# Hybrid decoder layer on one core: gate and up with seven block products in place of eight for three of eight pairs of k tiles

## The chip, the cores and the metric

The kernel runs on one core of a Trainium2 chip. The metric is the device time of one execution in microseconds. One core has a matrix engine (TensorE, in the profile PE, its weight loads PEld), three engines for elementwise work (VectorE or DVE, ScalarE or ACT, GpSimd or POOL) and an engine that issues most transfers (SyncE, SP). Matrix results land in PSUM, eight banks of 512 float32 columns on each of 128 partitions.

## The reference, cut to what matters

256 tokens of width 2048 go through a SwiGLU half step (inner width 5632), a two-branch mixer and a second SwiGLU half step:

```python
def swiglu(h, w_gu, w_down):
    g, u = jnp.split(h @ w_gu, 2, axis=-1)
    return (jax.nn.silu(g) * u) @ w_down

x = x + 0.5 * swiglu(rms_norm(x, g_ffn1[l]), w_gu1[l], w_down1[l])
x = x + hybrid_mixer(rms_norm(x, g_mix[l]), w_in[l], ...)
x = x + 0.5 * swiglu(rms_norm(x, g_ffn2[l]), w_gu2[l], w_down2[l])
```

All data is float32. The change lies in the two SwiGLU steps.

## The kernel before

Every float32 operand of a large product is split into two float32r parts, hi and lo, by `split` (L93): ScalarE casts hi (L95), VectorE subtracts to get lo (L96). A product is the sum of hi·hi, hi·lo and lo·hi. The weights pass through a `Feed`: SyncE fetches groups of 128 x 2048 (1 MB) into three raw buffers, and parts of 128 x 1024 are split into three pairs of hi and lo buffers. A part may be split once the part three places ahead of it has been used by TensorE, so the split runs at most two parts ahead of the products. Each engine works its instructions off in the order in which the program emits them; nothing is reordered.

There are two forms of product. `by_column` (L192) keeps the weights stationary: for each k tile of 128 and each block of 128 columns, one matmul of whi with both parts of the activations side by side (512 columns, L207) and one of wlo with the hi part (256 columns, L209, L206). `by_token` (L169) keeps the activations stationary and streams the weights: three matmuls of 512 columns (L185 to L187) for each k tile and each half of 128 tokens. Gate and up use `by_column`, 44 tiles of 256 columns (128 of gate, 128 of up) in each SwiGLU step, 16 k tiles each; down uses `by_token`, in two halves of 22 k tiles.

The 1/rms of the tokens is not needed for the first products: it is applied to their results (`scaled`, L252 to L256, by `rows`). So the rms is computed beside the first tiles. `pending` holds work for TensorE that is run between parts (one item per part), `posts` work for ScalarE and VectorE that is run when a part is taken.

PSUM is given out in rotation: `ps_mm` has two buffers of two banks for results, `ps_t` two banks for transposes, `ps_a` two single banks for attention.

Of the kernel before, what the change touches and what calls it, by code (L numbers as in the profile page):

```python
# [12 lines left out]
F32 = mybir.dt.float32  # L13
# [12 lines left out]
HALVES = 2  # L26
FKT = DFF // P // HALVES
# [12 lines left out]
NCH = 512  # L40
ND = D // NCH
RAW = 4 * NCH
SUB = 2 * NCH
BUFS = 3
WAKE = 8
# [4 lines left out]
def hybrid_layer(ctx: ExitStack, tc: tile.TileContext, a: dict, out: bass.AP):  # L50
# [50 lines left out]
    def transpose4(srcs, name):  # L101
        """srcs[t]: [128 tokens, 256 columns] -> PSUM [128 columns, 2, 256 tokens]"""
# [14 lines left out]
    class Feed:  # L117
        """The weights in the order of their use: fetched in groups, split part by part, both ahead of the products"""

        def __init__(self):  # L120
            self.groups, self.parts = [], []
            self.fetched = self.split = self.taken = 0
            self.raw, self.ready = {}, {}

        def add(self, dram, width, cuts=None, on_fetch=None, on_split=None):
            """dram: [128, width]; cuts: the widths of the parts where each is fetched by itself"""
            for c0 in range(0, width, RAW):
                n = min(RAW, width - c0)
                g, o, ws, whole = len(self.groups), 0, [], not cuts
                while o < n:  # L130
                    w = cuts.pop(0) if cuts else min(SUB, n - o)
                    ws.append(w)
                    self.parts.append((g, o, w, c0 + o, on_split))
                    o += w
# [15 lines left out]

        def take(self):
            while self.split < min(self.taken + BUFS, len(self.parts)):
                i = self.split
                self.split += 1
                g, o, w, col, hook = self.parts[i]
                self.fetch(g + BUFS)
                hi = wsplit.tile([P, SUB], F32R, tag="hi", name="hi")
                lo = wsplit.tile([P, SUB], F32R, tag="lo", name="lo")
                split((hi[:, :w], lo[:, :w]), self.raw[g][:, o:o + w])
                if hook:  # L160
                    hook(col, w)
                self.ready[i] = hi, lo, w
# [6 lines left out]
    def by_token(x, kts, name, step, apart=False):  # L169
        """x @ w, the activations stationary; step takes PSUM [128 tokens, 512] for both token blocks"""  # L170
# [6 lines left out]
        while k0 < kts:  # L177
            hi, lo, w = feed.take()
# [11 lines left out]
        posts.append(lambda: step(ps))  # L190

    def by_column(x, kts, name, *steps):  # L192
        """(x @ w)^T, the weights stationary; steps take SBUF [128 columns, 2 column blocks, 256 tokens]"""
        ps = ps_mm.tile([P, 2, NCH], F32, tag="mm", name=name)
        k0 = 0
        while k0 < kts:
            hi, lo, w = feed.take()
# [27 lines left out]
    def rsqrt(v, shape, name):  # L225
        """1 / sqrt(v), refined once"""
# [10 lines left out]
    class Norm:  # L237
        """h: (x * gain)^T in two parts; rows: 1/rms of every token along the free dimension"""

        def __init__(self, which):  # L240
            self.which = which
            self.h = keep.tile([P, NKD, 2, S], F32R, tag="h", name=f"h{which}")
# [29 lines left out]

    class NormOfColumns(Norm):
        """x^T comes from DRAM"""

        def __init__(self, which, xT, pool):
# [3 lines left out]
            self.sq = [pool.tile([P, 4, S], F32, name=f"sq{i}") for i in range(3)]  # L280
            self.acc = pool.tile([P, 4, S], F32, name="acc")

        def fetch(self, col, w):
            ks = slice(col // (2 * P), (col + w) // (2 * P))
            nc.sync.dma_start(self.xT[:, ks], self.dram[:, ks])

        def parts(self, col, w):
            for k in range(col // (2 * P), (col + w) // (2 * P)):
                self.part(k, self.xT[:, k])

        def stats(self, c):
            x = self.xT[:, 4 * c:4 * c + 4]
            dst = self.sq[c - 1] if c else self.acc
# [40 lines left out]
    def add_ffn(w_gu, w_down, first=None):  # L334
        for half in range(HALVES):
            for c in range(FKT):
                w, hooks = w_gu[half * FKT + c], {}
                if first and half == 0 and c == 0:
                    ks = (1, 1, 2, 2, 2, 2, 2, 2, 2)
                    hooks = dict(cuts=[k * 2 * P for k in ks], on_fetch=first.fetch, on_split=first.parts)  # L340
                if first and half == 0 and c == 1:
                    hooks = dict(cuts=[k * 2 * P for k in (2, 2, 4)])
                feed.add(w, NKD * 2 * P, **hooks)
            for n in range(ND):
                feed.add(w_down[half, n], FKT * NCH)
# [13 lines left out]
    def ffn(norm, fpool, first=None, after=None, late=(), out_rows=None):  # L359
        for half in range(HALVES):  # L360
            last = half == HALVES - 1
            act = fpool.tile([P, FKT, 2, S], F32R, tag="act", name="act")

            def gated(c, act=act):
                def gate(s):
                    sg = work.tile([P, S], F32, tag="sg", name="sg")
                    nc.scalar.activation(sg, s[:, 0], AF.Silu)
                    nc.vector.tensor_tensor(s[:, 0], s[:, 1], sg, op=ALU.mult)

                def parts(s):  # L370
                    split((act[:, c, 0], act[:, c, 1]), s[:, 0])

                return norm.scaled, gate, parts

            c0 = first(gated) if first and half == 0 else 0
            for c in range(c0, FKT):
                steps = gated(c)
                if half == 0 and c == 0:
# [358 lines left out]
```

## Time and profile before

| what | value |
|---|---|
| time before, median of 3 runs | 2096.28 us (2095.21 to 2096.97) |
| span of the profiled execution | 2094.5 us |
| TensorE busy | 2084.7 us, 100% of the span |
| VectorE busy | 1238.6 us, 59% |
| ScalarE busy | 982.9 us, 47% |
| weights read | 386 MB, 185 GB/s over the span |

The profile describes one execution; its span runs from the first to the last instruction, and no other time of that execution is listed beside it, so the span is what the profile gives. A busy TensorE is one that always has a matmul in its pipeline; the time that one costs is read from the distance of two starts, since each is shown longer than that (0.39 us shown, 0.23 us from start to start).

### The profile page before, as it was taken

The page shows a single profiled execution, that of the slowest core. Times are in us where ns is not written, and L with a number is a line of the kernel's source. Part 1 is how long each engine was busy: PE and PEld are TensorE (multiplying, and loading weights), DVE is VectorE, ACT ScalarE, POOL GpSimd, SP SyncE. Part 2 cuts the span into 40 slices and gives each one's busy share as a digit, 9 for nine tenths or more (in the row PEclk, how much of TensorE's full clock was granted, in tenths as well). Part 3 has the DMA queues.
Part 4 walks back from the last instruction along what each step waited for, and adds up shares of the span by engine and source line. Part 5 has one row for each costly group of instructions (what it writes and reads, how often), then busy time and mean ns, then how long its engine had stood idle before and what let it go on. Part 6 is the DMA issues. An engine that isn't in the chain of part 4 may idle for free.

```text
span 2094.5 us, 27027 instructions
## 1 busy us (share of the span) xinstructions
PE 2084.7 (100%) x10972; PEld 1771.2 (85%) x10972; DVE 1238.6 (59%) x1404; ACT 982.9 (47%) x1273; POOL 66.2 (3%) x55
## 2 busy tenths in 40 slices
PE   9999999999999999999999999999999999999999
PEld 8888888888888888877888888888888888888887
DVE  7656644556655555568666665565665445665544
ACT  6544433444444444445544444554444334444433
POOL 2000000000000000621000000000000000000000
PEclk9999999999999999999999999999999999999999
DMA  7655555655555555443555555555555555555564
GB/s 247 235 184 188 192 181 183 200 186 193 184 183 179 191 191 193 152 141 134 185 183 195 186 192 191 181 181 183 191 189 172 201 193 190 190 181 185 184 215 140
DMA packets 59246, 389.86 MB, mean 186 GB/s; under 512 B 7024, under 2 KB 7664, under 8 KB 13936
## 3 DMA queue, kind: packets, MB, share of 16 engines
q1 hardware_dynamic: 58976, 388.10, 55.3%
q8 instruction: 86, 1.41, 0.3%
q14 instruction: 40, 0.33, 0.0%
q10 hardware_dynamic: 144, 0.02, 0.0%
HBM read 386.00 MB, written 2.10 MB: 185 GB/s over the span
## 4 chain that ended last, share of the span: by engine, by line
PE 97%; POOL 1%; DMA 0%; DVE 0%; issue 0%; ACT 0%; SPq 0%; POOLq 0%; DVEq 0%; ACTq 0%
PE gu L207 31%; PE gu L209 15%; PE dn L187 8%; PE dn L186 8%; PE dn L185 8%; PE gate L207 6%; PE yo L207 3%; PE gate L209 3%; PE xc L207 2%; PE bg L207 2%; PE o L185 1%; PE o L187 1%; PE o L186 1%; PE yo L209 1%; PE qkv L187 1%; PE qkv L186 1%
## 5 line engine op out<-in xcount | busy, mean ns | idle before, releaser
L96 DVE TENSOR_TENSOR lo<-raw,hi 128x1024 fp32r<-128x1024 f32 (+1 forms) x734 | 912.7, 1244 | 793.8 <-ACT hi L95 784.5
L95 ACT CAST hi<-raw 128x1024 fp32r<-128x1024 f32 (+1 forms) x734 | 766.4, 1044 | 1003.1 <-PE gu L207 490.9
L207 PE MATMUL gu<-h,hi 128*128 128x512 f32 x2816 | 989.5, 398 | 1.0 <-DVE h L248 1.0
L209 PE MATMUL gu<-h,lo 128*128 128x256 f32 x2640 | 742.3, 281 | 0.4 <-DVE lo L96 0.4
L207 PEld LDWEIGHTS gu<-h,hi 128*128 128x128 f32 x2816 | 524.1, 188 | 123.7 <-DVE h L248 1.8
L209 PEld LDWEIGHTS gu<-h,lo 128*128 128x128 f32 x2640 | 499.4, 189 | 4.7 <-DVE lo L96 1.1
L187 PE MATMUL dn<-hi,act 128*128 128x512 f32 x704 | 277.1, 394 | 0.0
L186 PE MATMUL dn<-lo,act 128*128 128x512 f32 x704 | 275.5, 391 | 0.0
L185 PE MATMUL dn<-hi,act 128*128 128x512 f32 x704 | 274.4, 390 | 0.0
L207 PE MATMUL gate<-h,hi 128*128 128x512 f32 x512 | 179.2, 392 | 0.0
L186 PEld LDWEIGHTS dn<-lo,act 128*128 128x128 f32 x704 | 132.2, 188 | 30.5
L185 PEld LDWEIGHTS dn<-hi,act 128*128 128x128 f32 x704 | 132.2, 188 | 28.7
L187 PEld LDWEIGHTS dn<-hi,act 128*128 128x128 f32 x704 | 132.3, 188 | 27.1
L209 PE MATMUL gate<-h,lo 128*128 128x256 f32 x480 | 134.4, 280 | 0.0
L207 PEld LDWEIGHTS gate<-h,hi 128*128 128x128 f32 x512 | 95.9, 187 | 20.6 <-issue 0.8
L207 PE MATMUL xc<-h,hi 128*128 128x512 f32 x256 | 93.4, 407 | 0.0
L209 PEld LDWEIGHTS gate<-h,lo 128*128 128x128 f32 x480 | 90.7, 189 | 0.7
L209 PE MATMUL xc<-h,lo 128*128 128x256 f32 x240 | 67.9, 283 | 0.0
L254 DVE TENSOR_TENSOR gu_s<-gu_s,rows 128x512 f32<-128x512 f32 x88 | 60.9, 693 | 2.9
L218 DVE TENSOR_TENSOR gu_s<-gu,gu_t 128x512 f32<-128x512 f32 x88 | 60.3, 685 | 0.1
L207 PEld LDWEIGHTS xc<-h,hi 128*128 128x128 f32 x256 | 48.5, 191 | 12.9 <-issue 1.6
L216 ACT COPY gu_t<-gu 128x512 f32<-128x512 f32 x88 | 50.9, 578 | 0.0
(155 smaller groups left out, 1531.0 us busy)
## 6 DMA issues: line engine op xcount, KB each, us to landing
raw<-in_w_gu SPq DMA_DIRECT2D x173, 1024.0 KB, 5.0
raw<-in_w_down SPq DMA_DIRECT2D x80, 1024.0 KB, 4.9
raw<-in_w_mix SPq DMA_DIRECT2D x56, 1024.0 KB, 5.0
raw<-in_w_o SPq DMA_DIRECT2D x16, 1024.0 KB, 4.9
raw<-in_w_qkv SPq DMA_DIRECT2D x12, 1024.0 KB, 4.8
raw<-in_w_down SPq DMA_DIRECT2D x16, 512.0 KB, 3.5
raw<-in_w_oc SPq DMA_DIRECT2D x8, 1024.0 KB, 4.8
raw<-in_w_oa SPq DMA_DIRECT2D x8, 1024.0 KB, 4.9
```

The source lines that it names most:

```text
L95: nc.scalar.copy(dst[0], src)
L96: nc.vector.tensor_tensor(dst[1], src, dst[0].bitcast(F32), op=ALU.subtract)
L185: nc.tensor.matmul(ps[t], x[:, k, 0, ts], hi[:, js], start=k == 0, stop=False)
L186: nc.tensor.matmul(ps[t], x[:, k, 0, ts], lo[:, js], start=False, stop=False)
L187: nc.tensor.matmul(ps[t], x[:, k, 1, ts], hi[:, js], start=False, stop=k == kts - 1)
L207: nc.tensor.matmul(ps[:, b], whi, both, start=k == 0, stop=last)
L209: nc.tensor.matmul(ps[:, b, :S], wlo, x[:, k, 0], start=False, stop=False)
L216: nc.scalar.copy(t, ps[:, :, S:])
L218: nc.vector.tensor_tensor(s, ps[:, :, :S], t, op=ALU.add)
L254: engine.tensor_tensor(s, s, self.rows.unsqueeze(1).broadcast_to([P, 2, S]), op=ALU.mult)
```

## The change

It rewrites gate and up of both SwiGLU steps. The down projection keeps its form, and the mixer is not touched.

- **Order of the work.** A unit is 512 columns of gate and the same 512 of up; a SwiGLU step has 11 of them in groups of 4, 4 and 3 (`UNITS`), each group followed by its part of down. So down now has three passes over the residual in place of two.
- **Form of the product.** The activations are stationary and the weights stream, three matmuls of 512 columns for a product of one block (`product`). The four results (token half a or b, gate 0 or up 1) fill the four banks of `ps_mm` as a0, a1, b0, b1 (`plain`).
- **Seven products.** Where `PLAN` has an s (pairs 0, 3 and 5 of the 8 pairs of k tiles), the two k tiles, two token halves and gate/up form a product of 2 x 2 blocks, which `seven` does with seven block products (p1, p5, p6, p7 in banks of their own, the rest added to a0, a1, b0). It needs four sums of weight blocks (`sums`, VectorE, then split like weights) and three sums of activation blocks (`turn_into_forms`). `gather` and `combine` put the results together. The first unit of each step is plain throughout.
- **Normalised activations.** From the second unit on, h is multiplied by 1/rms in place, pair by pair (`turn_into_forms`), and split again. In the first step one pair is done at the end of the first unit and the others during the second; in the second step all are done during the first unit.
- **Transposes.** The results have tokens on the partitions, and down needs columns there: eight transposes per unit on TensorE (`turns`).
- **Feed.** Parts of units after the first may use two more buffers from a pool of the step (`MORE`), so up to four parts are split ahead.

The diff, cut to its core:

```diff
+UNITS = (4, 4, 3)
+PAIRS = NKD // 2
+PLAN = "sppspspp"
+MORE = 2
...
+        def sums(self, raw):
+            b = raw.rearrange("p (b n) -> p b n", n=NCH)
+            u = self.u = self.pool.tile([P, 4, NCH], F32, tag="u", name="u")
+            nc.vector.tensor_tensor(u[:, :2], b[:, 0:4:3], b[:, 1:2].broadcast_to([P, 2, NCH]), op=ALU.add)
+            nc.vector.tensor_tensor(u[:, 2], u[:, 0], b[:, 3], op=ALU.add)
+            nc.vector.tensor_tensor(u[:, 3], u[:, 2], b[:, 2], op=ALU.add)
...
+                if len(own) < BUFS:
+                    home = wsplit
+                elif form and self.pool and len(self.homes) - len(own) < MORE:
+                    home = self.pool
...
+        def turn_into_forms(self, p, pool):
+            k = 2 * p
+            h = self.h[:, k:k + 2]
+            t = pool.tile([P, 2, S], F32, tag="rn", name="rn")
+            nc.vector.tensor_tensor(t, h[:, :, 0].bitcast(F32), h[:, :, 1].bitcast(F32), op=ALU.add)
+            nc.vector.tensor_tensor(t, t, self.rows.unsqueeze(1).broadcast_to([P, 2, S]), op=ALU.mult)
+            if PLAN[p] == "s":
+                f = pool.tile([P, 3, P], F32, tag="rf", name="rf")
+                a11, a21, a12, a22 = t[:, 0, :P], t[:, 0, P:], t[:, 1, :P], t[:, 1, P:]
+                nc.vector.tensor_tensor(f[:, 0], a22, a21, op=ALU.subtract)
+                nc.vector.tensor_tensor(a21, a11, a21, op=ALU.subtract)
+                nc.vector.scalar_tensor_tensor(f[:, 1], a21, -1.0, a22, op0=ALU.mult, op1=ALU.subtract)
+                nc.vector.tensor_tensor(f[:, 2], a12, f[:, 1], op=ALU.add)
+                self.forms[p] = pool.tile([P, 2, 3, P], F32R, tag=f"forms{p}", name=f"forms{p}")
+                split((self.forms[p][:, 0], self.forms[p][:, 1]), f)
+            split((h[:, :, 0], h[:, :, 1]), t)
...
+        def product(self, name, x, hi, lo, last):
+            ps = self.bank(name)
+            nc.tensor.matmul(ps, x[0], hi, start=name not in self.begun, stop=False)
+            nc.tensor.matmul(ps, x[0], lo, start=False, stop=False)
+            nc.tensor.matmul(ps, x[1], hi, start=False, stop=last)
...
+        def seven(self, p, last):
+            for names in (("p5", "p7"), ("p6", "b0"), ("a0", "a1"), ("p1",)):
+                hi, lo, _, _ = feed.take()
+                for j, name in enumerate(names):
+                    js = slice(j * NCH, (j + 1) * NCH)
+                    self.product(name, x[name], hi[:, js], lo[:, js], last and name[0] == "p")
+                run(pending)
...
+        def combine(self):
+            g, v, a, b = self.g, self.v, self.banks["a"], self.banks["b"]
+            nc.vector.tensor_tensor(g[:, 1], g[:, 1], b[:, 0], op=ALU.add)
+            nc.vector.tensor_tensor(v[:, 1], b[:, 1], v[:, 1], op=ALU.subtract)
+            nc.vector.tensor_tensor(g[:, 0], g[:, 0], a[:, 0], op=ALU.add)
+            nc.vector.tensor_tensor(v[:, 0], a[:, 1], v[:, 0], op=ALU.subtract)
+            nc.scalar.activation(g, g, AF.Silu)
+            posts.append(lambda: nc.vector.tensor_tensor(g, g, v, op=ALU.mult))
...
+                    while col + w < end:
+                        hi, lo, w, col = feed.take()
+                        unit.plain(hi, lo, w, col, col + w == end)
+                        run(pending)
+                        if norm.spread_done and late_pool and 2 * (norm.turned + 1) * SUB <= col + w:
+                            norm.turn_into_forms(norm.turned, late_pool)
+                            norm.turned += 1
+                    run(posts, len(posts))
+                    unit.direct()
...
+                    for p in range(PAIRS):
+                        if norm.turned <= p:
+                            norm.turn_into_forms(norm.turned, late_pool)
+                            norm.turned += 1
+                        if PLAN[p] == "s":
+                            unit.seven(p, "s" not in PLAN[p + 1:])
```

**Where a unit ends and the next begins.** On VectorE, a tile of gate and up looked like this before (`lo` is a part of the weights, `gu_s` the results of the tile in SBUF, `rows` the 1/rms):

```order
L218 TENSOR_TENSOR gu_s<-gu,gu_t 128x512
L254 TENSOR_TENSOR gu_s<-gu_s,rows_122 128x512
L96 TENSOR_TENSOR lo<-raw,hi 128x1024
L368 TENSOR_TENSOR gu_s<-gu_s,sg 128x256
L96 TENSOR_TENSOR lo<-raw,hi 128x1024
L96 TENSOR_TENSOR act<-gu_s,act 128x256
L96 TENSOR_TENSOR lo<-raw,hi 128x1024 x2
```

Now, from the last two act splits of one unit to the first sums for pair 3 of the next (`at` are the transposed results, `gu` the banks a and b, `g` and `v` the gate and up results in SBUF, `u` the sums of weights):

```order
L99 TENSOR_TENSOR act<-at,act 128x2x256 x2
L476 TENSOR_TENSOR g<-g,gu 128x512
L477 TENSOR_TENSOR v<-gu,v 128x512
L478 TENSOR_TENSOR g<-g,gu 128x512
L479 TENSOR_TENSOR v<-gu,v 128x512
L99 TENSOR_TENSOR lo<-raw,hi 128x1024
L481 TENSOR_TENSOR g<-g,v 128x1024
L99 TENSOR_TENSOR lo<-raw,hi 128x1024 x3
L167 TENSOR_TENSOR u<-raw 128x1024
L168 TENSOR_TENSOR u<-u,raw 128x512
L169 TENSOR_TENSOR u<-u,raw 128x512
L99 TENSOR_TENSOR lo<-u,hi 128x1024 x2
```

The four reads of the PSUM banks (L476 to L479) stand behind the splits for the next unit's pair 0, and the next unit's parts behind them and the multiplication (L481).

**Where the first unit of the first step ends.** Before, the rows behind the rms (`diag` holds it) were splits of weights and the results of the first tiles:

```order
L264 TENSOR_SCALAR diag<-ident,rs_y 128x128 x2
L96 TENSOR_TENSOR lo<-raw,hi 128x1024 x3
L218 TENSOR_TENSOR gu_s<-gu,gu_t 128x512
L254 TENSOR_TENSOR gu_s<-gu_s,rows_122 128x512
L368 TENSOR_TENSOR gu_s<-gu_s,sg 128x256
L96 TENSOR_TENSOR lo<-raw,hi 128x1024
```

Now, from the last splits for pair 0 of the second unit on (`rn` are the normalised activations, `rf` and `forms` their sums, `h` the activations themselves, `raw` the weights):

```order
L99 TENSOR_TENSOR lo<-raw,hi 128x1024
L99 TENSOR_TENSOR lo<-raw,hi 128x512
L315 TENSOR_TENSOR rn<-h_124 128x512
L316 TENSOR_TENSOR rn<-rn,rows_125 128x512
L320 TENSOR_TENSOR rf<-rn 128x128
L321 TENSOR_TENSOR rn<-rn 128x128
L322 SCALAR_TENSOR_TENSOR rf<-rn 128x128
L323 TENSOR_TENSOR rf<-rn,rf 128x128
L99 TENSOR_TENSOR forms_526<-rf,forms_526 128x384
L99 TENSOR_TENSOR h_124<-rn,h_124 128x2x256
L490 SCALAR_TENSOR_TENSOR g<-gu,rs_y,g 128x512 x2
L99 TENSOR_TENSOR lo<-raw,hi 128x1024 x4
```

The forms of pair 0, then the results of the first unit (L490), then four splits stand ahead of pair 1's activations, which come next in the queue.

**Where the first unit of the second step ends.** At this place the rows before were those of the first piece above. Now, around the last two pairs of activations:

```order
L99 TENSOR_TENSOR lo<-u,hi 128x1024 x2
L315 TENSOR_TENSOR rn<-h_9876 128x512
L316 TENSOR_TENSOR rn<-rn,rows_9877 128x512
L99 TENSOR_TENSOR h_9876<-rn,h_9876 128x2x256
L99 TENSOR_TENSOR lo<-raw,hi 128x1024
L99 TENSOR_TENSOR lo<-raw,hi 128x512
L315 TENSOR_TENSOR rn<-h_9876 128x512
L316 TENSOR_TENSOR rn<-rn,rows_9877 128x512
L99 TENSOR_TENSOR h_9876<-rn,h_9876 128x2x256
L490 SCALAR_TENSOR_TENSOR g<-gu,rs_y,g 128x512 x2
L99 TENSOR_TENSOR lo<-raw,hi 128x1024 x4
L167 TENSOR_TENSOR u<-raw 128x1024
```

The read of the first unit's PSUM banks (L490) stands behind both pairs of activations and the splits for the second unit.

## Rows read from the trace of the kernel before

**Rows 1.** The page: span, busy time of each engine.
```profile
span 2094.5 us, 27027 instructions
...
PE 2084.7 (100%) x10972; PEld 1771.2 (85%) x10972; DVE 1238.6 (59%) x1404; ACT 982.9 (47%) x1273; POOL 66.2 (3%) x55
```

**Rows 2.** The chain that ended last, first and last of eighteen tile borders: start, us, what.
```profile
54.63 0.46 PE gu L207 x2
...
246.73 0.45 PE gu L207 x2
```

**Rows 3.** Timeline of TensorE, first down projection: its first matmul and the next stage's.
```profile
258.10 0.40 PE L185 MATMUL dn<-hi,act 128*128 128x512 f32 x1
...
378.96 0.40 PE L207 MATMUL gu<-h,hi 128*128 128x512 f32 x1
```

**Rows 4.** Timeline of TensorE, q/k/v projection: first and last of 197 matmuls.
```profile
769.83 0.39 PE L187 MATMUL qkv<-hi,h 128*128 128x512 f32 x1
...
814.25 0.39 PE L185 MATMUL qkv<-hi,h 128*128 128x512 f32 x1
```

**Rows 5.** Timeline of TensorE: four transposes between matmuls of the down projection.
```profile
663.08 0.60 PE L106 MATMUL xt<-ident,x_res 128*128 128x128 f32 x4
...
663.44 0.47 PE L185 MATMUL dn<-hi,act 128*128 128x512 f32 x1
...
663.75 0.39 PE L186 MATMUL dn<-lo,act 128*128 128x512 f32 x1
```

**Rows 6.** Timeline of VectorE, gate and up; idle time before and its releaser in brackets.
```profile
59.88 1.22 DVE L96 TENSOR_TENSOR lo<-raw,hi 128x1024 fp32r<-128x1024 f32 x1
...
61.02 0.42 DVE L368 TENSOR_TENSOR gu_s<-gu_s,sg 128x256 f32<-128x256 f32 x1
...
64.38 1.23 DVE L96 TENSOR_TENSOR lo<-raw,hi 128x1024 fp32r<-128x1024 f32 x1 [1.27 <-ACT hi L95]
...
68.46 0.69 DVE L218 TENSOR_TENSOR gu_s<-gu,gu_t 128x512 f32<-128x512 f32 x1
...
69.18 0.69 DVE L254 TENSOR_TENSOR gu_s<-gu_s,rows 128x512 f32<-128x512 f32 x1
```

**Rows 7.** Timeline of VectorE, other stages.
```profile
926.05 0.68 DVE L528 SCALAR_TENSOR_TENSOR pr<-sc,mask 128x512 f32<-128x512 f32 x1
...
926.65 1.21 DVE L96 TENSOR_TENSOR lo<-raw,hi 128x1024 fp32r<-128x1024 f32 x1
...
1363.57 0.15 DVE L325 TENSOR_REDUCE ssqs<-ssq 128x2 f32<-128x8 f32 x1
...
1365.19 0.48 DVE L264 TENSOR_SCALAR diag<-ident,rs_y 128x128 f32<-128x128 f32 x2
...
1365.59 1.22 DVE L96 TENSOR_TENSOR lo<-raw,hi 128x1024 fp32r<-128x1024 f32 x1
```

**Rows 8.** Timeline of ScalarE, gate and up.
```profile
60.47 1.06 ACT L95 CAST hi<-raw 128x1024 fp32r<-128x1024 f32 x1
...
63.30 1.05 ACT L95 CAST hi<-raw 128x1024 fp32r<-128x1024 f32 x1 [1.43 <-PE gu L207]
```

**Rows 9.** Groups by line and shape: count, busy us, mean ns, idle before.
```profile
L95 ACT CAST m<-yo_s 128x512 fp32r<-128x512 f32 x8 | 5.0, 622 | 5.0 <-DVE yo_s L646 5.0
...
L367 ACT ACT_TABLE_LOAD x2 | 2.6, 1283 | 0.0
```

**Rows 10.** Timeline, the last matmul of the program and what reads its result.
```profile
2090.38 0.40 PE L187 MATMUL dn<-hi,act 128*128 128x512 f32 x1
...
2090.82 0.69 DVE L388 SCALAR_TENSOR_TENSOR x_res<-dn,x_res 128x512 f32<-128x512 f32 x1 [0.68 <-PE dn L187]
```

**Rows 11.** Timeline of TensorE: the longest wait.
```profile
863.43 0.55 PE L106 MATMUL qp<-ident,qall 128*128 128x128 f32 x3 [3.13 <-POOL qall L496]
```

**Rows 12.** Windows behind that wait; PEclk is the granted clock.
```profile
864.00:866.00 2.00, 2.00 (x9) 1.72 (x9) 0.42 (x1) 1.53 (x2) 1.92 (x3) 0.61 0.00 0
...
866.00:868.00 2.00, 2.00 (x9) 1.71 (x8) 1.75 (x1) 0.00 (x0) 1.92 (x2) 0.53 0.00 0
```

More of the change, by code (lines that the diff above doesn't have):

```diff
@@ L40 @@
 NCH = 512
+UKT = NCH // P
 ND = D // NCH
@@ L129, in add @@
                 g, o, ws, whole = len(self.groups), 0, [], not cuts
+                if plan and plan[c0 // RAW] == "s":
+                    for form in "ud":
+                        self.parts.append((g, 0, SUB, c0, None, form))
+                    self.parts.append((g, SUB, SUB, c0, None, "r"))
+                    self.parts.append((g, 0, NCH, c0, None, "r"))
+                    o = n
                 while o < n:
@@ L167, in hybrid_layer, with by_token @@
     feed = Feed()
-    def by_token(x, kts, name, step, apart=False):
+    def by_token(x, kts, name, step, apart=False, hold=posts):
         if apart:
@@ L177, in by_token @@
         while k0 < kts:
-            hi, lo, w = feed.take()
+            hi, lo, w, _ = feed.take()
             nk = w // NCH
@@ L189, in by_token @@
             run(pending)
-        posts.append(lambda: step(ps))
+        hold.append(lambda: step(ps))
     def by_column(x, kts, name, *steps):
@@ L334, in add_ffn @@
     def add_ffn(w_gu, w_down, first=None):
[L335 to L343, printed above, removed]
+        u0 = 0
+        for units in UNITS:
+            for u in range(u0, u0 + units):
+                hooks = dict(plan=PLAN if u else None)
+                if first and u == 0:
+                    cuts = [NCH, NCH] + [SUB] * 7
+                    hooks = dict(cuts=cuts, on_fetch=first.fetch, on_split=first.parts)
+                feed.add(w_gu[u], NKD * SUB, **hooks)
             for n in range(ND):
-                feed.add(w_down[half, n], FKT * NCH)
+                feed.add(w_down[n, :, u0 * UKT * NCH:(u0 + units) * UKT * NCH], units * UKT * NCH)
+            u0 += units
     def add_mixer():
@@ L392, in add @@
                         after(n)
-                by_token(act, FKT, "dn", add, apart=final and n == ND - 1)
+                by_token(act, units * UKT, "dn", add, apart=final and n == ND - 1)
     box = {}
@@ L662, in hybrid_layer, with open_late @@
     norm3 = box[2]
-    with tc.tile_pool(name="ffn2", bufs=1) as fpool:
-        ffn(norm3, fpool, out_rows=out)
+    with tc.tile_pool(name="ffn2", bufs=1) as fpool, ExitStack() as later:
+        def open_late():
+            feed.pool = later.enter_context(tc.tile_pool(name="late2", bufs=1))
+            return feed.pool
+        ffn(norm3, fpool, open_late, out_rows=out)
         run(posts, len(posts))
```

193 lines of the change are left out of this document (140 added, 53 removed).

## The prediction

> **What bounds the kernel now.** I read the page first: TensorE is busy for 2084.7 of 2094.5 us, VectorE for 59% and ScalarE for 47% [rows 1]. So the time is the sum of TensorE's matmuls, and the first question is what a matmul costs from start to start. In the chain, eighteen borders between gate/up tiles stand from 54.63 to 246.73 us [rows 2]; seventeen tiles in 192.10 us are 11.30 us each, and 44 tiles are 497.2 us in each SwiGLU step. The down projection, whose form gate and up now take, shows its price between its first matmul and the next stage: 528 matmuls from 258.10 to 378.96 us, 0.229 us each [rows 3]. The q/k/v projection has the same form and runs slightly faster, 196 distances in 44.42 us, 0.2266 us [rows 4]. I take 0.229 and keep 0.2266 as the other bound.
>
> **What TensorE saves.** A plain unit is 16 k tiles x 4 blocks x 3 = 192 matmuls, 43.95 us; one with three s pairs has 3 x 3 fewer, 183, 41.89 us. A step has one and ten of them: 462.8 us against 497.2. Two steps save 68.7 us. The transposes come on top: four of them move the second matmul behind them to 663.75 us, where without them it would start at 663.08 + 0.23 = 663.31 [rows 5], so four cost 0.44 and the eight of a unit 0.88 us; 22 units make 19.4. Net: **-49.3 us**, if TensorE never waits.
>
> **What VectorE then has to do.** Its prices, from start to start: 1.14 us for 128x1024 (59.88 to 61.02) and 0.72 for 128x512 where the next reads its result (68.46 to 69.18) [rows 6]; 0.60 for an independent 128x512 (926.05 to 926.65) and 0.20 for 128x128 (two in 0.40) [rows 7]; 128x384 lies between, I estimate 0.47. A steady unit has 23 operations of 1024 (19 weight parts, 3 first sums, the multiplication) and 19 of 512: 26.2 + 11.4 us, plus 0.12 each for 8 dependent ones: 38.6 us, against 42.8 on TensorE (41.89 + 0.88). ScalarE has 1.05 us per cast [rows 8] and is far from full. VectorE fits, with 90% in place of 61%, so the question is where its queue holds TensorE up. All times below start at the end of a unit on TensorE.
>
> *Between two units.* VectorE can read a result 0.44 us after the last matmul's start [rows 10], 0.2 after its slot ends. Four reads of 0.60 end at 2.6. Bank b is due after nine matmuls (2.06) and free at 1.5; a is due at 2.75 and free at 2.7: no wait. But ScalarE's silu (1024 columns, by the cast 1.06 [rows 8]) stands ahead of the cast for pair 1: third read done 2.05, silu done 3.2, cast 4.25, subtraction 5.5. TensorE wants it for its second matmul at 5.04. About 0.45 us, fourteen times: **+6**. If VectorE's queue were longer, it would be late here first.
>
> *From a unit to down.* Down takes a buffer of `ps_mm` with its first matmul, the one of b, free at 1.5 us. Six times: **+9** (at least 4, if the first read alone frees it). *From down to a unit:* the buffer of a waits for the residual's two additions, which stand behind a cast and a subtraction (2.2 us): free at 3.45, due at 2.75; four times 0.7: **+3**.
>
> *The second unit of the first step.* Here the forms are made while they are needed. A plain pair costs VectorE 0.60 + 0.72 + 0.60 = 1.9 us; an s pair has four operations of 128 more (4 x 0.20 + 4 x 0.12 = 1.28) and one of 384, 3.7; and inside each it waits for a cast of 0.62 [rows 9]. TensorE sums the squares two parts, 5.5 us, before the unit ends; the chain to the rms took 2.0 us (1363.57 to 1365.59 [rows 7]); then VectorE's queue holds the sums (2.6), three subtractions (3.4) and a short one (0.6), so it is free at 3.2. Pair 0's forms are cast 0.60 + 0.72 + 1.28 + 0.5 later, by 6.2 (the 0.5 an estimate from the 0.62), where TensorE would have begun at 0. The table load (1.28 us [rows 9]) and silu put the read of the first unit's banks at 9.3 where 8.4 was due. Pair 0 ends at 12.0 instead of 4.8. Pair 1's activations come after four subtractions: 16.8, a wait of 4.7. Then by the same rows, pair after pair: 0.8 at pair 2, 1.0 within pair 3, 5.1 at pair 4, 0.6 within pair 5, 3.5 at pair 6, and 0.5 of waits for low parts. The unit ends at 65.9 in place of 42.8: **+23**. Its lower bound is VectorE's work alone, 46 us up to the last weight part, without the waits for casts: +15; the upper one adds a late next unit, +27.
>
> *The first unit of the second step.* Its bank b is free only when the last residual is added, behind a cast and a subtraction: 3.45 instead of 0.69, +2.8. Then five pairs of forms follow in five parts. In each part VectorE's loop is subtraction, form, wait for the casts, next part: 4.2 us for a plain pair, 5.7 for an s pair, against 2.75 on TensorE: 24.0 against 13.8, of which the lead of two parts covers about 3.3: +7. Last, the read of its banks stands far back in the queue: from 4.2 us before the unit's end VectorE has 2.6 of sums, 4.0 of subtractions, two pairs with their casts (5.1), then table load, silu and the read itself (2.5). That is 10.0 where 2.06 was due, +8: **+18** in all, at least 10 without the casts.
>
> *The start of the program.* First parts are larger (256 KB in place of 128), but the first 8 MB of weights need half of the xT rate they needed. No row prices it; I take 0, between -2 and +3.
>
> *The clock.* After a wait of 3.13 us [rows 11] the granted clock was 0.61 and 0.53 in the next two windows [rows 12], the lower level, 1.2 GHz, for most of them: 2 x 0.39 + 2 x 0.47 = 1.7 us lost. By the Trainium skill (TensorE: Matmul & The Clock Gate, HAM oscillation) idle gaps between bursts of matmuls throttle the engine again. The trace agrees: 0.53 behind 3.13 us without a matmul. Four waits above are longer than 3.13 us: 6.8, but in the second unit TensorE waits for VectorE again anyway, so **+3**.
>
> **The sum:** -49.3 + 6 + 9 + 3 + 23 + 18 + 3 = +12.7 us on the span, 2107.2. The median of the runs is 1.8 above the span; so **2109 us**, slower by 0.6%. A measurement can tell about 0.2%, 4 us.
>
> **Rivals.**
> - *The casts hold nothing up (faster).* One mechanism, at the two starts: if ScalarE has each form cast by the time VectorE asks, the two starts cost 15 and 10 instead of 23 and 18, and without the long waits the 3 for the clock is gone: 2109 - 19 = 2090. For it: ScalarE has room (47% [rows 1]). Against: cast and subtraction are a chain, 63.30 to 64.38 us in the trace even where both engines are idle [rows 6, 8]. It decides once the two starts together cost less than 24 us.
> - *VectorE becomes the bound in every unit (slower still).* If an operation costs its shown length, 1.23 and 0.69, and not the distance, VectorE needs 23 x 1.23 + 19 x 0.69 = 41.4 us in a unit, and laid out as above a unit takes 44.6 in place of 43.2: 18 units, +25, and 2134. Against: the starts of 59.88 and 61.02 lie 1.14 apart [rows 6]. The Trainium skill (VectorE: DVE Perf Modes, The DRAIN you can't avoid) says that the next operation does not start until the pipeline is empty, which would be this rival; the rows show it starting 0.08 us before the shown end. A slower fetch would look the same.
> - *The lead hides it all (much faster).* Four parts ahead are up to 11 us of TensorE's work. If that covered the two starts and the borders, the sum is -49.3 and 2047. Against: in both starts the lead is used up in the order of the queue itself, and the reads of banks have no lead.
> - *The matmuls run as in q/k/v.* 4044 x 0.0023 = 9.3 us less: 2100, no change that can be told. For it: the same stationary operand, h.
>
> **How the numbers follow.** My forecast: 0.46, with its own range 2098 to 2122. Casts hidden: 0.21. VectorE the bound: 0.15. All hidden: 0.07. As q/k/v: 0.11. The range for 8 in 10 goes from 2080, under the first rival, to 2136, over the second; it leaves out the 0.07 of all hidden and some of the second's upper part. Faster by over 0.2% (under 2092): 0.28. Slower by over 0.2% (above 2100.5): 0.60. Within: 0.12.
>
> **What the profile after will show.** If I am right: TensorE busy for about 2030 us plus waits, its waits listed at L436 and L437 for VectorE and ScalarE, most of them in two stretches of some 50 us, behind the first unit of each step; steady units of 43 us; VectorE near 90% in them; a wait of about 1.5 us at L221 at six places. Wrong would be: matmuls of the units at another distance than 0.229, steady units of 44 us or more with VectorE never idle, or the second unit of the first step near 45 us.

## The result and the profile after

The changed kernel takes **2131.25 us** (median of 4 runs, 2130.35 to 2132.15) against 2096.43: 1.0168 times the time before, interval 1.0154 to 1.0183. It is slower by 34.8 us where 12.6 were forecast. The first lines of its page, which answer to [rows 1]:

```profile
span 2129.2 us, 24288 instructions
PE 2067.4 (97%) x9560; PEld 1687.9 (79%) x9560; DVE 1513.2 (71%) x1669; ACT 1027.3 (48%) x1234; POOL 64.3 (3%) x55
```

TensorE is no longer always busy. What it waited for (total us, times, longest):

```profile
PE dn L221 <- DVE v L477: 8.8, 6, 1.5
PE gu L437 <- DVE lo L99: 8.2, 10, 1.7
PE gu L436 <- DVE g L490: 8.1, 1, 8.1
PE gu L436 <- ACT hi L98: 7.2, 5, 3.9
PE p L436 <- ACT forms L98: 5.9, 1, 5.9
PE gu L436 <- DVE x_res L562: 3.8, 4, 1.0
PE gu L436 <- ACT h L98: 3.7, 1, 3.7
```

These are the places that the prediction named. To price them, the borders of units are read from TensorE's timeline: the start of the program, the second unit of the first step, a steady unit (one behind the second unit of a step), and the first two units of the second step.

```profile
4.83 0.48 PE L436 MATMUL gu<-hi,h 128*128 128x512 f32 x1
...
57.09 0.39 PE L438 MATMUL gu<-hi,h 128*128 128x512 f32 x1
...
63.83 0.80 PE L436 MATMUL p<-hi,forms 128*128 128x512 f32 x1 [5.91 <-ACT forms L98]
...
127.16 0.39 PE L436 MATMUL p<-hi,forms 128*128 128x512 f32 x1
...
392.10 0.39 PE L436 MATMUL p<-hi,forms 128*128 128x512 f32 x1
...
435.80 0.39 PE L436 MATMUL p<-hi,forms 128*128 128x512 f32 x1
...
1371.53 0.39 PE L436 MATMUL gu<-hi,h 128*128 128x512 f32 x1
...
1429.42 0.39 PE L436 MATMUL p<-hi,forms 128*128 128x512 f32 x1
1431.27 0.40 PE L438 MATMUL p<-hi,forms 128*128 128x512 f32 x1
1439.76 0.80 PE L436 MATMUL gu<-hi,h 128*128 128x512 f32 x1 [8.08 <-DVE g L490]
...
1483.25 0.40 PE L436 MATMUL p<-hi,forms 128*128 128x512 f32 x1
```

The steady unit has 43.70 us; the eighteen of them have 43.3 to 43.9, 784.8 together. The busy time of the engines in the steady unit shown, in two stretches of the first step, and behind the wait of 8.1 us (busy time and number for PE, PEld, VectorE, ScalarE and GpSimd, then TensorE's granted clock, where 1.00 is the upper level, 2.4 GHz, and 0.5 the lower, 1.2 GHz; then the share and rate of the transfers):

```profile
392.10:435.80 43.70, 43.47 (x192) 35.00 (x191) 39.13 (x43) 23.30 (x26) 0.00 (x0) 1.00 0.51 193
50.00:75.00 25.00, 15.67 (x60) 12.32 (x59) 20.85 (x33) 13.61 (x18) 0.00 (x0) 0.86 0.44 156
75.00:100.00 25.00, 20.07 (x72) 14.99 (x73) 20.94 (x32) 8.92 (x13) 0.00 (x0) 0.87 0.19 75
1430.00:1455.00 25.00, 16.92 (x63) 13.20 (x62) 18.71 (x22) 12.98 (x15) 0.00 (x0) 0.80 0.34 126
```

Before the change, the first matmuls of the two steps and of the second step's down stood here (timeline of the kernel before):

```profile
4.95 0.77 PE L207 MATMUL gu<-h,hi 128*128 128x512 f32 x1
1350.52 0.39 PE L207 MATMUL gu<-h,hi 128*128 128x512 f32 x1
1600.48 0.40 PE L185 MATMUL dn<-hi,act 128*128 128x512 f32 x1
```

So its first 22 tiles (248.6 us at 11.30) lost 4.5 us in the first step, up to 258.10 [rows 3], and 1.4 in the second. With this the terms of the forecast can be set beside what the trace shows ("distance" is from the start of one matmul to the start of the next):

| term | forecast | measured | from |
|---|---|---|---|
| matmuls and transposes | -49.3 | -44.9 | mean distance 0.2302 us in 20 units, not 0.229 |
| unit to unit, 14 times | +6 | +9.5 | 784.8 - 18 x 183 x 0.2302 - 14 x 0.88 = 14.2, less the next but one line |
| unit to down, 6 times | +9 | +10.3 | 1.71 at each first matmul of down |
| down to unit, 4 times | +3 | +4.7 | 1.19 each |
| second unit, first step | +23 | +26.9 | 127.16 - 57.32 = 69.84, less 42.77 and the 0.2 of the distance |
| start of the second step | +18 | +23.4 | 1483.25 - 1371.53 = 111.72, less 43.95 + 42.77, 0.2, and the 1.4 of before |
| start of the program | 0 | +3.9 | 57.32 - 4.83 - 43.95 = 8.5, less the 4.5 of before and 0.1 for the earlier start |
| lower clock | +3 | in the lines above | some 55 matmuls of the first two units of both steps, about 0.427 us apart, 10.8 us too long |
| sum | +12.7 | +33.8 | the span grew by 34.7 |

No term has another sign than forecast, and no single one holds the missing 22 us; seven are too small, by 1.3 to 5.4 us, and 0.9 us of the span stay without a place.

### The profile page after: what moved, and what is told of

Read it like the earlier page. It is cut to its first block, busy times and chain, and to the rows that moved or that the text cites. A ratio compares the mean times of both kernels' runs of the same rounds, so it can differ in the third digit from the quotient of the medians.

```text
span 2129.2 us, 24288 instructions
## 1 busy us (share of the span) xinstructions
PE 2067.4 (97%) x9560; PEld 1687.9 (79%) x9560; DVE 1513.2 (71%) x1669; ACT 1027.3 (48%) x1234; POOL 64.3 (3%) x55
## 4 chain that ended last, share of the span: by engine, by line
PE 88%; DVE 6%; ACT 2%; issue 2%; POOL 1%; DMA 1%; SPq 0%; ACTq 0%; DVEq 0%; POOLq 0%
PE gu L437 10%; PE gu L438 10%; PE gu L436 10%; PE dn L221 8%; PE dn L223 8%; PE dn L222 7%; PE gate L243 5%; DVE lo L99 3%; PE yo L243 3%; PE gate L245 3%; PE p L436 2%; PE p L437 2%; PE p L438 2%; PE xc L243 2%; ACT hi L98 2%
## 5 line engine op out<-in xcount | busy, mean ns | idle before, releaser
L99 DVE TENSOR_TENSOR lo<-raw,hi 128x1024 fp32r<-128x1024 f32 (+1 forms) x729 | 868.6, 1203 | 525.0 <-ACT hi L98 517.5
L98 ACT CAST hi<-raw 128x1024 fp32r<-128x1024 f32 (+1 forms) x729 | 728.0, 1012 | 631.9 <-PE dn L223 253.0
L436 PE MATMUL gu<-hi,h 128*128 128x512 f32 x1048 | 418.7, 399 | 29.2 <-DVE g L490 8.1
L437 PE MATMUL gu<-lo,h 128*128 128x512 f32 x1048 | 417.3, 398 | 9.0 <-DVE lo L99 8.2
L438 PE MATMUL gu<-hi,h 128*128 128x512 f32 x1048 | 414.3, 395 | 0.0
L221 PE MATMUL dn<-hi,act 128*128 128x512 f32 x704 | 278.7, 396 | 8.8 <-DVE v L477 8.8
L436 PEld LDWEIGHTS gu<-hi,h 128*128 128x128 f32 x1048 | 198.9, 190 | 84.6 <-issue 12.8
L437 PEld LDWEIGHTS gu<-lo,h 128*128 128x128 f32 x1048 | 198.9, 190 | 61.7 <-DVE lo L99 19.4
L98 ACT CAST hi<-u 128x1024 fp32r<-128x1024 f32 x120 | 126.2, 1052 | 229.7 <-DVE u L167 183.2
L438 PEld LDWEIGHTS gu<-hi,h 128*128 128x128 f32 x1048 | 198.9, 190 | 45.1 <-DVE h L285 0.8
L221 PEld LDWEIGHTS dn<-hi,act 128*128 128x128 f32 x704 | 132.3, 188 | 37.4 <-issue 11.2
L99 DVE TENSOR_TENSOR lo<-u,hi 128x1024 fp32r<-128x1024 f32 x120 | 146.5, 1222 | 3.4 <-ACT hi L98 0.3
L167 DVE TENSOR_TENSOR u<-raw 128x1024 f32<-128x1024 f32 x60 | 73.1, 1218 | 0.0
```

What stands on the lines that cost most here:

```text
L167: nc.vector.tensor_tensor(u[:, :2], b[:, 0:4:3], b[:, 1:2].broadcast_to([P, 2, NCH]), op=ALU.add)
L221: nc.tensor.matmul(ps[t], x[:, k, 0, ts], hi[:, js], start=k == 0, stop=False)
L436: nc.tensor.matmul(ps, x[0], hi, start=name not in self.begun, stop=False)
L437: nc.tensor.matmul(ps, x[0], lo, start=False, stop=False)
L438: nc.tensor.matmul(ps, x[1], hi, start=False, stop=last)
```

## The experiments

### What the seven products and the starts are worth

**e1_all_plain.** `PLAN` without an s; the unit's banks are read directly.

```diff
-PLAN = "sppspspp"
+PLAN = "pppppppp"
...
+        def read(self):
...
+            for t in range(TB):
+                nc.scalar.activation(g[:, t], self.banks["ab"[t]][:, 0], AF.Silu)
+            for t in range(TB):
+                nc.vector.tensor_tensor(g[:, t], self.banks["ab"[t]][:, 1], g[:, t], op=ALU.mult)
...
-                    unit.combine()
+                    unit.read()
```

> All eight pairs plain, normalised in place as in the changed kernel; the banks are read directly by silu and the multiplication. Against the changed kernel at 2131: twenty units have 9 matmuls more, at 0.230 us +41. The sums of weights (2.3 us of VectorE for each s pair) are gone, VectorE falls from 90% to about 65% in a unit, and a pair's forms cost it 1.9 us, not 3.7. Theory 1 (the two starts, the borders and the clock hold the loss; the seven products give their full saving): second unit of the first step from 27 us of loss to about 12, first two units of the second step from 25 to about 15, each unit's first product now waits for a silu of a bank, about +1 at 16 borders: 2131 + 41 - 25 + 16, about 2160. Theory 2 (VectorE's load is the bound and the seven products save little): about 2131 or less. The distance of matmuls tells a third thing: 0.229 again if VectorE's load had stretched it to 0.230.

2160.8 us (1.0306 of before, 1.029 to 1.0321), as theory 1 gave. The seven products do save what they should; VectorE's load did not eat them. The time alone would not show it, since e1 has borders of its own; but a steady unit of it takes 46.0 us (343.18 to 389.18) against 43.7, and of these 2.3 us nine matmuls at 0.230 us are 2.1. The distance is 0.2296 and 0.2299 in two of its units, though VectorE has 54% of the span there, so 0.0008 of the 0.0013 us above down's do not hang on its load.

**e2_unscaled and e5_unscaled_forms.** The forms are made of the unscaled activations; h stays as it is, and 1/rms goes on behind.

```diff
-            nc.vector.tensor_tensor(t, t, self.rows.unsqueeze(1).broadcast_to([P, 2, S]), op=ALU.mult)
-            split((h[:, :, 0], h[:, :, 1]), t)
...
-            nc.scalar.activation(g, g, AF.Silu)
+            for t in range(TB):
+                nc.scalar.activation(g[:, t], g[:, t], AF.Silu, scale=self.norm.rstd[:, t:t + 1])
...
+                    nc.vector.scalar_tensor_tensor(
+                        g[:, t], v[:, t], self.norm.rstd[:, t:t + 1], g[:, t], op0=ALU.mult, op1=ALU.mult
+                    )
```

> The activations are not normalised in place: the forms of the three s pairs are made from the unscaled h and 1/rms goes on at the silu (scale, two of 512 columns) and at the multiplication (two of 512). So plain pairs need no work, an s pair needs 2.35 us of VectorE in place of 3.7, and no form waits for the rms. Theory 1 (the rewriting of h is what the two starts wait for): the second unit of the first step falls from 27 us of loss to about 12 (the read of the first unit's banks stays, about 6, and three forms of 2.35 us on a VectorE that is full), the first two units of the second step from 25 to about 13 (five waits of 1 to 3 us gone, the wait for the banks down from 8 to 5): 2131 - 27 = 2104, between 2096 and 2112. Theory 2 (the weight parts and their casts are late by themselves when the fourfold lead is used up): over 2120.

> As e2_unscaled, with a11 - a21 as a fourth part of an s pair's forms (p7's stationary operand), so that the whole product is computed; a form's cast and subtraction have 512 columns in place of 384, 0.13 us more of VectorE for each of six forms. Theory 1 (the rewriting of h in place is what the two starts wait for): as e2_unscaled, 2099 to 2101. Theory 2 (the weight parts are late by themselves): over 2120.

e2 gives p7 the unchanged second token half, so that this half of the output is not the reference's; 2099.1 us. e5 computes all of it: **2098.3 us** (1.0008, 0.9999 to 1.0017). So 33 us, nearly the whole loss, hang on the rewriting of h. e5 takes out its work on VectorE, its casts and its wait for 1/rms together and does not tell these apart. The second unit of the first step loses 7.4 us in place of 27.1, the start of the second step 6.4 in place of 25.0. What is left to wait for:

```profile
PE dn L221 <- DVE v L474: 8.8, 6, 1.5
PE gu L434 <- DVE lo L99: 8.7, 19, 1.7
PE gu L433 <- DVE x_res L567: 3.8, 4, 1.0
```

The forms and the 8.1 us for the read of the banks (g) are gone from the head of the list. Some 4 us are given back in the steady units (43.73 for the one of 43.48): there are two silus of 512 columns now in place of one of 1024, and two multiplications.

### The lower clock

**e3_filled_waits and e6_zero_fills.** Matmuls with a stationary operand of zeros stand ahead of the five long waits. The cut is e6's; in e3 the moving operand is a part of h.

```diff
+FILLS = {0: 22, 1: 14, 4: 14, 6: 4}
...
+        def fill(self, name, n):
+            ps = self.bank(name)
+            for _ in range(n):
+                nc.tensor.matmul(ps, feed.zero[:, :P], feed.zero, start=name not in self.begun, stop=False)
+                self.begun.add(name)
...
+                    if name == "b0" and p == 0 and self.fills == 2:
+                        self.fill("p6", 32)
...
+                        if unit.fills == 1 and p in FILLS:
+                            unit.fill("p5" if p < 6 else "a0", FILLS[p])
```

> Nothing is removed: 54 matmuls with a stationary operand of zeros (512 columns, added to sums that they leave as they are) stand ahead of the four long waits of the first step's second unit (22, 14, 14 and 4) and 32 ahead of the wait of 8 us in the second step. The changed kernel shows some 55 matmuls 0.427 us apart behind these waits, 0.2 us each too long, 11 us. Theory 1 (the lower clock behind a wait is paid in full): no distances of 0.427 there any more and about 2131 - 11 = 2120. Theory 2 (in the first step's second unit TensorE waits for VectorE again anyway, so a slower matmul only shortens the next wait; only what follows the last wait counts, 1.8 and 2.4 us): distances of 0.229 but about 2127. Theory 3 (the lower clock does not come from idleness): distances of 0.427 stay, 2131 or more.

> As e3_filled_waits, but the filling matmuls read nothing but zeros, so they wait for nothing and end before the wait does: 22, 14, 14 and 4 in the first step's second unit, 32 in the second step's. Theory 1 (the lower clock is paid in full): 2131 - 10 = 2121. Theory 2 (in the second unit TensorE waits for VectorE anyway; only the slow matmuls behind the last wait count, 1.6 us there and 2.4 in the second step, a little more as the unit's last pairs have a lead): no distances of 0.427 from 57 to 130 us or behind 1440 us, and 2125 to 2128.

e3 missed: its filling matmuls read h as the moving operand and waited for the rewriting of h themselves (6.0 us in the second step, and the 32 of them then ran behind the wait): 2136.3. In e6 they read zeros alone:

```profile
50.00:75.00 25.00, 22.36 (x99) 17.31 (x98) 21.77 (x39) 13.71 (x18) 0.00 (x0) 1.00 0.41 141
75.00:100.00 25.00, 21.74 (x86) 15.84 (x87) 20.54 (x33) 9.29 (x13) 0.00 (x0) 1.00 0.25 92
1430.00:1455.00 25.00, 24.12 (x106) 19.36 (x105) 18.91 (x22) 13.42 (x16) 0.00 (x0) 1.00 0.40 137
```

The granted clock is 1.00 in these stretches, where it was 0.80 to 0.87 (some 15 slow matmuls are left, 8 of them in the first unit, which got no filling), and the time is 2129.2 us (1.0156, 1.0142 to 1.0169), 2 us less and within the interval of the changed kernel. This is nearest to theory 2, though 1 us above its range: from its first matmul to its transposes the second unit is only 0.8 us shorter, since a faster matmul only waits longer for the next form; in the second step, from the end of the wait to the transposes, it is 2.5 us, and there it counts.

### The borders

**e4_down_bank.** Down's first tile takes the banks of p5 and p7.

```diff
-                by_token(act, units * UKT, "dn", add, apart=final and n == ND - 1)
+                by_token(act, units * UKT, "dn", add, apart=n == 0 or final and n == ND - 1)
```

> The first tile of down in each pass takes the two single banks that p5 and p7 have left, in place of the buffer of b. Theory 1 (the wait of 1.6 us at the first matmul of down is for the bank alone): six waits gone, 2131 - 10 = 2121. Theory 2 (what VectorE owes at that place is late for the next one instead, the transposes of the last unit two parts later): 2128 to 2131, with new waits at the transposes.

2122.1 us (1.0124, 1.0107 to 1.0141): 9.2 us, theory 1; the six waits at L221 are gone from the list, and nothing at the transposes took their place.

**e11_silu_later.**

```diff
-            nc.scalar.activation(g, g, AF.Silu)
+            posts.append(lambda: nc.scalar.activation(g, g, AF.Silu))
```

> The changed kernel with one edit: the silu of a unit emitted behind the cast for the next part, the multiplication one part later. Theory 1 (the border between two units is the silu on ScalarE ahead of that cast): 0.5 us at 14 borders of unit and unit, 2131 - 7 = 2124, more if down's first steps gain too. Theory 2 (VectorE's four reads are the border): 2131, and the 10 us by which e7_three_edits is under the sum of its parts need another reason.

2128.4 us (1.0151, 1.0136 to 1.0166), between both theories and not told apart from the changed kernel by the intervals; but its steady units have 43.17, 43.39 and 43.5 us where there were 43.48, 43.70 and 43.85. So the silu is about half of a border, 0.33 of 0.69 us. The rest is the wait for VectorE's last read of bank a (0.18 and 0.24 us, with 0.2 to 0.3 of distance around it).

**e7_three_edits.** e5, e4 and the silu later.

> e5_unscaled_forms and e4_down_bank together, and the silu of a unit emitted behind the cast for the next part in place of ahead of it. The first two are at different places, so they should add: 2100 - 9 = 2091. The silu: a wait of about 0.3 us for the low part of pair 1 stands at each of 14 borders; theory 1 (it is the silu on ScalarE ahead of that cast): 4 us more, 2087. Theory 2 (VectorE's own queue is late there): nothing, 2091.

**2079.4 us** (0.9918, 0.9904 to 0.9932), faster than both kernels and than expected. The edits add: a pass of down with its borders falls from 90.51 to 88.81 us (10.2 in six), and the silu is worth more here (8.8 us over the 18 steady units), where there are two of them.

### The start of the program

**e9_squares_later.** On top of e7:

```diff
-            for c in range(4):
-                pending.extend((lambda c=c: norm1.stats(c), *[skip] * c))
-            pending[:0] = [skip] * 3
+            for c, n in enumerate((3, 1, 2, 2)):
+                pending.extend((*[skip] * n, lambda c=c: norm1.stats(c)))
+            pending.append(skip)
```

> e7_three_edits with the squares of xT emitted later in the first unit (after parts 4, 6, 9 and 12 in place of 4, 5, 7 and 10). In the changed kernel ScalarE stands 1.2, 3.2 and 6.4 us before squares whose xT is still on its way, with casts of weights queued behind, and the unit takes 8.5 us more than its matmuls. Theory 1 (the casts behind the squares are late): the waits at 28.7 and 38 to 42 us go, and the lower clock behind them: 3 to 4 us off, 2076. Theory 2 (VectorE's subtractions take 2.6 us there in place of 1.2, beside GpSimd's additions of the squares, and this moves along with them): 2079.

**2074.5 us** (0.9894, 0.9878 to 0.9911), 4.8 less than e7; the first unit has 48.6 us in place of 53.7, where the profiles of all kernels with the old order have 51.4 to 54.2. What stood there in the changed kernel, in ScalarE's, VectorE's and GpSimd's timelines:

```profile
25.39 1.06 ACT L350 ACTIVATE sq<-xT 128x1024 f32<-128x1024 f32 x1 [3.19 <-DMA xT<-in_xT]
26.36 1.03 ACT L98 CAST hi<-raw 128x1024 fp32r<-128x1024 f32 x1
36.88 1.06 ACT L350 ACTIVATE sq<-xT 128x1024 f32<-128x1024 f32 x1 [6.38 <-issue]
37.84 1.03 ACT L98 CAST hi<-raw 128x1024 fp32r<-128x1024 f32 x1
```

```profile
27.43 2.67 DVE L99 TENSOR_TENSOR lo<-raw,hi 128x1024 fp32r<-128x1024 f32 x1 [2.93 <-ACT hi L98]
30.41 1.21 DVE L99 TENSOR_TENSOR lo<-raw,hi 128x1024 fp32r<-128x1024 f32 x1
```

```profile
26.61 2.40 POOL L352 TENSOR_TENSOR acc<-acc,sq 128x1024 f32<-128x1024 f32 x1 [5.12 <-ACT sq L350]
```

ScalarE stands before a square whose xT is not there (the last part of it lands at 36.8 us), the casts behind it are late, and the subtraction that then starts beside GpSimd's addition takes twice its time. Which of the two counts is seen in e9, where the subtraction is still nearly twice as long:

```profile
31.28 2.42 POOL L349 TENSOR_TENSOR acc<-acc,sq 128x1024 f32<-128x1024 f32 x1 [5.74 <-ACT sq L347]
32.53 2.25 DVE L99 TENSOR_TENSOR lo<-raw,hi 128x1024 fp32r<-128x1024 f32 x1 [1.10 <-ACT hi L98]
```

No square waits for xT any more, and between 11 us and the end of the first unit TensorE waits for nothing, where it had three waits, 3.6 us, in the changed kernel. So it was the late casts, theory 1.

### How far VectorE is from being the bound

**e8_sums_on_gpsimd.** The three sums of `sums` as `nc.gpsimd.tensor_tensor` in place of `nc.vector`.

> The changed kernel with the three sums of weights of each s pair on GpSimd, which does 128x1024 in 2.4 us and 128x512 in 1.3 where it adds squares and scales results. VectorE loses 7 of its 39 us in a unit. Theory 1 (VectorE's queue holds TensorE up, at the starts and the borders, and stretches the matmuls by 0.0013 us): second unit of the first step 27 to about 20, the read of banks in the second step 8 to about 5.5, distances back to 0.229 (-5), borders -3: 2131 - 17 = 2114. Theory 2 (a sum on GpSimd ends 5 us after its data, and ScalarE's cast for it holds up the casts behind it; or both engines slow each other down): 2131 or more, with waits for hi at p.

2188.3 us (1.0437, 1.0423 to 1.0451): theory 2; which of its two reasons weighs more is not told apart. VectorE's and GpSimd's groups there (busy us, mean ns):

```profile
L99 DVE TENSOR_TENSOR lo<-raw,hi 128x1024 fp32r<-128x1024 f32 x667 | 945.0, 1425 | 527.6 <-ACT hi L98 522.4
```

```profile
L167 POOL TENSOR_TENSOR u<-raw 128x1024 f32<-128x1024 f32 x60 | 162.3, 2705 | 1320.5 <-DMA raw<-in_w_gu 1278.4 <-DVE lo L99 30.9 <-PE ssq L361 11.2
L169 POOL TENSOR_TENSOR u<-u,raw 128x512 f32<-128x512 f32 x60 | 120.9, 2015 | 4.7
```

The subtraction has a mean of 1425 ns where it had 1251, and the waits for it become TensorE's longest (44.4 us at L437). What a lighter VectorE would be worth by itself is therefore not shown.

**e10_four_sevens.** e7 with `PLAN = "spspspsp"`.

> e7_three_edits with four s pairs (spspspsp) in place of three; for its memory p7's stationary operand is written back into h instead of a fourth part of the forms. Each unit has 3 x 3 minus 6, that is 3 matmuls fewer, 0.69 us, 20 units: 14 us. VectorE gets 4.3 us more per unit (three sums, one and a half parts more): 38.7 + 4.3 = 43.0 where TensorE needs 42.2. Theory 1 (VectorE is then the bound): units of 43.0 to 43.5, nothing won, 2079 to 2083. Theory 2 (TensorE still is): 2066.

2122.0 us (1.012, 1.0105 to 1.0136). A unit of it:

```profile
384.20:429.90 45.70, 43.47 (x189) 34.17 (x189) 43.43 (x50) 25.25 (x29) 0.00 (x0) 1.00 0.52 184
```

This is 39 us above even theory 1. VectorE is busy for 43.4 of 45.7 us, more than the 42.2 that TensorE's work needs: with a fourth s pair VectorE is the bound, and nothing can be won against the 43.1 to 43.5 us of e7's steady units. The unit is longer by 2.3 us than with three, though it has 3 matmuls fewer, because TensorE also waits for the reads at the unit's start (0.8 and 0.3 us) and, as `gather` now stands right in front of the transposes, there (0.4 and 0.7). Another place of four s pairs was not tried, so only the first part is shown to be a limit.

**e12_switch_banks.** The two inner loops of `by_token` exchanged.

> The changed kernel, with the loops over token halves and k tiles exchanged in by_token, so that down, q/k/v and o change the PSUM bank after 3 matmuls, as the units do, and not after 6. In the changed kernel the mean distance of two matmuls is 0.2302 in a unit and 0.2289 in down. Theory 1 (the change of bank costs the difference): down at about 0.230, 2 to 3 us more in all. Theory 2 (it is something else in a unit): down stays at 0.229, 2131.

2130.1 us, down at 0.2289 as before: theory 2. Why the matmuls of a unit are 0.0013 us further apart than those of down stays open.

## Why the prediction was right and wrong, point by point

- **What bounds the kernel, and the sign.** Right: all of TensorE's time counted, the saving was there (e1), and more was lost at the starts and borders than it brought. Its own range ended at 2122; that the wide one holds 2131 is owed to a rival with another mechanism (2134), and so is luck, not the sum.
- **The step that failed is the sizing of the sum's terms,** from the best row of each: seven were too small, and the sum came to +12.7 where +34.7 was measured. The largest misses are the borders together (6.5), the start of the second step (5.4), the price of a matmul (4.4), the second unit and the start of the program (3.9 each). Told one by one:
- **Start of the second step, +18, measured +23.4.** The mechanism was right in every part: 2.9 us for x_res, then the loop of subtraction, form and cast at 4.2 us a part for plain pairs (TensorE waits at 1401.4, 1405.6, 1411.5, 1415.7 and 1422.8), then the read of the banks 8.1 us late where 8 was said. One turn of the loop on VectorE:

```profile
1401.37 1.23 DVE L99 TENSOR_TENSOR lo<-raw,hi 128x1024 fp32r<-128x1024 f32 x1 [0.26 <-ACT hi L98]
1402.52 0.68 DVE L315 TENSOR_TENSOR rn<-h 128x512 f32<-128x512 f32 x1
1403.23 0.69 DVE L316 TENSOR_TENSOR rn<-rn,rows 128x512 f32<-128x512 f32 x1
1404.61 0.69 DVE L99 TENSOR_TENSOR h<-rn,h 128x512 fp32r<-128x512 f32 x1 [0.69 <-ACT h L98]
1405.56 1.23 DVE L99 TENSOR_TENSOR lo<-raw,hi 128x1024 fp32r<-128x1024 f32 x1 [0.26 <-ACT hi L98]
```

  Too small were the waits of the five pairs (8.8, not 7: the lead covers less) and what the lower clock costs behind the last wait (2.2, booked apart).
- **Second unit of the first step, +23, measured +26.9,** at its upper bound of 27. First wait 6.3 us (6.2 forecast), second 3.9 (4.7), the one at pair 4 with its low parts 5.5 (5.1 and 0.5), at pair 6 2.5 (3.5). The waits together are 18.6 us, less than forecast; slow matmuls make up the rest. Pair 6 begins 55.2 us behind the end of the first unit, where the forecast's own waits give 53.9; so 2.6 of the 3.9 are lost behind that: 1.3 on its low part, the rest mostly on matmuls at the lower clock, which were booked apart.
- **The clock, +3.** 10.8 us of slow matmuls look like a term of their own, but e6 gives back 2.0 by the runs' medians, 0.8 + 2.5 by the two units in its trace: the 3 was right, because TensorE waits for VectorE in the second unit anyway, as the prediction said. By the Trainium skill (TensorE: Matmul & The Clock Gate, HAM oscillation) gaps between bursts throttle the engine again; the trace agrees (0.86 in the stretch with the wait of 5.91 us, 0.80 in the one with 8.08), and e6 shows that filling the gaps keeps the clock and yet hardly the time.
- **The borders, 18 in all, measured 24.5.** Unit to down was right and of the cause named (e4). Unit to unit: 0.69 us in place of 0.45. The silu is half of it (e11); the last read of bank a, which I had free at 2.7 us where 2.75 was due, is late by 0.2 to 0.3.
- **The price of a matmul, 0.229 taken from down [rows 3], measured 0.2302.** 4.4 us; neither VectorE's load (e1) nor the change of banks (e12) explains more than a part of it, and the cause stays open.
- **Start of the program, 0, measured +3.9.** I looked at the transfers and not at the order in ScalarE's queue, where the squares now stand ahead of their xT (e9). Before, all of xT had landed at 16.2 us and the first square started at 20.78.
- **The rivals.** Casts hidden: no, the chain of cast and subtraction runs as priced, and the two starts cost 50.3 together, not under 24. All hidden and as in q/k/v: no, by the waits and by 0.2302. VectorE the bound in every unit (2134): its time is near, but not its mechanism; VectorE has 39.1 us in a steady unit of 43.7, and e10 shows what a unit looks like when it is the bound. The Trainium skill's rule for it (VectorE: DVE Perf Modes, The DRAIN you can't avoid) is that the next operation does not start until the pipeline is empty, but that one which is not held starts earlier. A steady unit shows both. The second of two subtractions from sums (`u`) starts 1.28 us behind the first, which takes 1.22 (2.50 for the two); the raw one behind them starts at 407.21, 0.08 before their end at 407.29, as after the raw one of [rows 6]:

```profile
404.79 2.50 DVE L99 TENSOR_TENSOR lo<-u,hi 128x1024 fp32r<-128x1024 f32 x2
407.21 1.82 DVE L99 TENSOR_TENSOR lo<-raw,hi 128x1024 fp32r<-128x1024 f32 x2
```

- **The signs named at the end of the prediction.** Right: six waits of up to 1.5 us at L221, the waits in two stretches behind the first units, VectorE at 90% of a steady unit (39.13 of 43.70). TensorE is busy for 2067.4 us, not about 2030: the longer distance and the slow matmuls are some 15 of that, the rest is not broken down. Of the signs of being wrong one came: a distance other than 0.229.

## What to carry to other kernels

The sums over two token halves are taken apart again in the results, so a scale per token can go on behind them: form them from the unscaled operand, and no form waits for the scale or has to be written back. Read the order of an engine's queue for what stands behind each wait before pricing a transfer or a clock: three edits of order or place and one of algebra turned 1.7% slower into 1.1% faster with the same matmuls. And where many terms are laid end to end, each from its best row, their errors need not cancel: here seven of eight were too small.

## What the runs showed of the hardware that was not expected

- VectorE and GpSimd hold each other up. In the changed kernel the addition of GpSimd at 26.61 ends at 29.01; the subtraction that starts at 27.43 ends at 30.10, 1.09 us behind it, where such a one takes 1.21 alone. The same at 38.08: GpSimd ends at 40.45, the subtraction of 38.90 (2.62 us) at 41.52. By the Trainium skill (SBUF — State Buffer, SBUF: two separate sides) the two share one pair of ports under a lock, and an operation of VectorE with two inputs in SBUF and one of GpSimd that reads SBUF block each other for a whole instruction; these rows agree. It goes both ways: before the change three additions in a row beside four subtractions took 3.06 us each, where the mean of the three is 2.39 in the changed kernel, and the subtractions 2.63:

```profile
23.82 9.18 POOL L296 TENSOR_TENSOR acc<-acc,sq 128x1024 f32<-128x1024 f32 x3 [21.51 <-ACT sq L294]
24.70 10.52 DVE L96 TENSOR_TENSOR lo<-raw,hi 128x1024 fp32r<-128x1024 f32 x4 [0.67 <-ACT hi L95]
```

  With 180 additions on GpSimd the mean subtraction goes from 1251 to 1425 ns (e8).
- A full granted clock need not be worth much: 1.00 in place of 0.86 over 50 us made the unit 0.8 us shorter (e6), because TensorE then waited longer for VectorE.
